# Softmax difference of a differential attention: three engines share the step that two did

## The chip, the cores and the metric

The kernel runs on one core of a Trainium2 chip. The metric is device time of one execution in microseconds (us); lower is better. The core's engines run side by side, each through its own fixed queue of instructions, and wait for one another by semaphores: TensorE (PE in the profile; its weight loads are PEld), VectorE (DVE), ScalarE (ACT), GpSimd (POOL) and SyncE (SP), which issues all transfers here.

## The reference

One layer of a streaming encoder: RMSNorm, one input projection whose columns feed an attention group and a gated convolution, an output projection, a residual and a final RMSNorm. The change concerns the attention of 2048 prompt frames, which has two softmaxes for each of 4 heads and subtracts them:

```python
def diff_attend(q, k, v, q_pos, k_pos, lam, rel_bias):
    s = jnp.einsum('bqhcd,bkhcd->bchqk', q, k, preferred_element_type=f32) * SCALE
    bias = rel_bias[rel_bucket(k_pos[None, :] - q_pos[:, None])]
    s = s + jnp.transpose(bias, (2, 0, 1)).astype(f32)[None, None]
    vis = chunk_id(k_pos)[None, :] <= chunk_id(q_pos)[:, None]
    s = jnp.where(vis, s, NEG)
    p = jax.nn.softmax(s, axis=-1)
    a = p[:, 0] - lam * p[:, 1]
    return jnp.einsum('bhqk,bkhd->bqhd', a.astype(v.dtype), v)
```

## The kernel before, in words

The frames are taken in four parts `p` of 512. For each part and head `h`, `unit_a` makes queries, keys, values and the gate by projections (`proj`, L217 is their matmul), `attend` does the attention, and `unit_c` does a quarter of the convolution. Every projection splits its weights into a high and a low half: ScalarE casts `wr` to `wh` (L196), GpSimd (VectorE for some columns) subtracts to get `wl` (L197), and three matmuls take the place of one.

`attend` goes through a part's four tiles of 128 queries, in two pairs. The keys that a tile sees (16 meta tokens and all frames up to its own) are cut into 1 to 5 chunks of at most 512 columns. There are 64 tiles and 176 chunks. For each chunk and each of the two components, `softmax_diff` does this:

- two matmuls write negated scores to PSUM (`s`, L438 and L439, three buffers),
- VectorE takes each row's minimum `nm` (L388; L385 with the bias for the last chunk),
- ScalarE writes the exponentials to SBUF (L389): component 0 to a tile `p0`, component 1 to a tile `p1` (12 and 6 buffers), and adds up each row.

Then `coefs` makes from minima and sums one factor for each row, chunk and component, `cf` (L362 to L369, small instructions on VectorE and one on ScalarE). The factor of component 1 contains minus lambda. The last loop scales both and adds them into `p0`; it is the place of the change. Back in `attend`, TensorE transposes `p0` block by block into PSUM (`pt`, L454), ScalarE casts that to `ah` (L457), VectorE subtracts to get `al` (L458), and TensorE multiplies with the values (`po`, L461 to L463). Other lines in the prediction: L297 takes the values from PSUM to SBUF before their transposes (L308), L180 is in the gate's `softplus_neg`, L532 scales a convolution input by the norm on GpSimd, L144 casts the input on ScalarE, and L686 is the matmul of the output projection, whose first half is laid among the last tiles.

The program is written head after head. A scheduler, which runs when the program is built, sets the order of each engine's queue, so that projections stand between the matmuls of the attention; a change in one place moves instructions elsewhere too.

Of the kernel before, what the change touches and what calls it, by code (L numbers as in the profile page):

```python
# [13 lines left out]
AF = mybir.ActivationFunctionType  # L14
ALU = mybir.AluOpType
# [32 lines left out]
def hybrid_step(ctx: ExitStack, tc: tile.TileContext, x, xT, ckT, cv, scT, rel_bias, norm_g, w_in,  # L48
# [10 lines left out]
    op = pool("op", 3)  # L59
# [9 lines left out]
    V, S, G, T = nc.vector, nc.scalar, nc.gpsimd, nc.tensor  # L69
# [281 lines left out]
    def coefs(nm, l, nch, pn, lam=None):  # L351

        n = nm.shape[1]
        lam = lam2 if lam is None else lam
        cf = sm.tile([P, 2, 5], F32, tag="cf", name="cf")[:pn, :n, :nch]
        r = sm.tile([P, 2], F32, tag="r2", name="r2")[:pn, :n]
        if nch == 1:
            V.reciprocal(cf, l)
            V.tensor_tensor(cf, cf, lam[:pn].unsqueeze(2), op=ALU.mult)
            return cf  # L360
        M = sm.tile([P, 2], F32, tag="M2", name="M2")[:pn, :n]
        V.tensor_reduce(M, nm, op=ALU.min, axis=AX.X)  # L362
        V.tensor_tensor(nm, nm, M.unsqueeze(2).broadcast_to([pn, n, nch]), op=ALU.subtract)
        S.activation(nm, nm, AF.Exp, scale=-1.0)
        V.tensor_tensor(l, l, nm, op=ALU.mult)
        V.tensor_reduce(M, l, op=ALU.add, axis=AX.X)
        V.reciprocal(r, M)
        V.tensor_tensor(r, r, lam[:pn], op=ALU.mult)  # L368
        V.tensor_tensor(cf, nm, r.unsqueeze(2).broadcast_to([pn, n, nch]), op=ALU.mult)  # L369
        return cf  # L370

    def softmax_diff(pn, chunks, mm, bz):


        nch = len(chunks)
        nm = sm.tile([P, 2, 5], F32, tag="nm", name="nm")[:pn, :, :nch]
        l = sm.tile([P, 2, 5], F32, tag="l", name="l")[:pn, :, :nch]
        pr = []
        for j, (c0, w) in enumerate(chunks):
            pr.append([pp.tile([P, 512], F32, tag=f"p{c}", name=f"p{c}", bufs=NP[c])[:pn, :w] for c in range(2)])  # L380
            for c in range(2):
                s = ps_s.tile([P, 512], F32, tag="s", name="s")[:pn, :w]
                mm(c, s, c0, w)
                if j == nch - 1:
                    V.tensor_tensor_reduce(s, s, bz[:, 512 - w:], 1.0, BIG, ALU.add, ALU.min,  # L385
                                           accum_out=nm[:, c, j:j + 1])
                else:
                    V.tensor_reduce(nm[:, c, j:j + 1], s, op=ALU.min, axis=AX.X)  # L388
                S.activation(pr[j][c], s, AF.Exp, bias=nm[:, c, j:j + 1], scale=-1.0, accum_out=l[:, c, j:j + 1])  # L389
        cf = coefs(nm, l, nch, pn)  # L390
        for j, (a0, a1) in enumerate(pr):
            G.tensor_scalar(a0, a0, cf[:, 0, j:j + 1], 1.0, op0=ALU.mult, op1=ALU.mult)  # L392
            V.scalar_tensor_tensor(a0, a1, cf[:, 1, j:j + 1], a0, op0=ALU.mult, op1=ALU.add)  # L393
        return [a0 for a0, _ in pr]

    def chunks_of(t):
# [28 lines left out]
    def attend(h, p, st):  # L425
# [5 lines left out]
        for b in range(2):  # L431
            tl = [4 * p + 2 * b, 4 * p + 2 * b + 1]
            aa = []
            for t in tl:
                qs = slice(P * (t - 4 * p), P * (t - 4 * p + 1))

                def mm(c, ps, col, w):
                    T.matmul(ps, lhsT=qd[c][0][:, qs], rhs=ks[c][:, col:col + w], start=True, stop=False)  # L438
                    T.matmul(ps, lhsT=qd[c][1][:, qs], rhs=ks[c][:, col:col + w], start=False, stop=True)  # L439
                ch = chunks_of(t)  # L440
                aa.append((ch, softmax_diff(P, ch, mm, st["bz"])))
# [364 lines left out]
```

## Time and profile before

| | |
|---|---|
| median of 3 runs | 1325.93 us (1325.57 to 1329.85) |
| profiled execution | 1329.5 us, of which the span from first to last instruction 1327.7 us |
| busy: TensorE, VectorE, ScalarE, GpSimd | 97%, 75%, 56%, 55% |
| granted TensorE clock | 0.99 |

In a group of instructions the profile gives the line, the engine, the operation, what is written and read, the shape and the count, then busy us, mean ns of one, the engine's idle time ahead of them, and what ended it. `(+5 forms)` means that the group has other shapes too. A line of waits reads: who waited, for whom, us in total, how many times, the longest.

### The profile page before, as it was taken

The numbers are of one execution on the slowest core, as the hardware profiler recorded it, in microseconds if no ns is written. First come the engines' busy times: TensorE is split into PE (matmuls) and PEld (weight loads), VectorE is DVE, ScalarE is ACT, GpSimd is POOL, SyncE is SP. The second block draws the span as 40 slices with busy tenths as digits, with TensorE's granted clock in tenths as the row PEclk, the third lists the DMA queues.
The fourth block names the chain that finished last, engine by engine and source line by source line (L and its number), as shares of the span: only waits on it lengthen the run. The fifth ranks groups of instructions, "written<-read, shape, count | busy, mean of one in ns | idle before, by whom it ended". The sixth has DMA issues, their size and how long they took to land.

```text
span 1327.7 us, 21145 instructions
## 1 busy us (share of the span) xinstructions
PE 1281.4 (97%) x7058; PEld 1105.9 (83%) x7058; DVE 1000.8 (75%) x2086; ACT 740.3 (56%) x1854; POOL 732.1 (55%) x659
## 2 busy tenths in 40 slices
PE   8999999999899999999999999999999999999897
PEld 6999999978788887888888887878888888888675
DVE  7756667657798858898969867788788897856653
ACT  6645453564556547566655565565656675654221
POOL 5675655556466665466656745566567575543100
PEclk9999999999999999899999999999999999999999
DMA  9743533764334447444353453444334434567741
GB/s 296 214 146 95 161 90 97 221 212 151 113 111 136 144 136 234 155 135 143 97 167 115 140 183 103 120 137 126 103 105 152 143 120 137 165 196 255 223 159 52
DMA packets 108045, 198.72 MB, mean 150 GB/s; under 512 B 17408, under 2 KB 45600, under 8 KB 107936
## 3 DMA queue, kind: packets, MB, share of 16 engines
q1 hardware_dynamic: 107936, 197.37, 48.0%
q8 instruction: 55, 0.90, 0.3%
q14 instruction: 54, 0.44, 0.1%
HBM read 145.62 MB, written 43.26 MB: 142 GB/s over the span
## 4 chain that ended last, share of the span: by engine, by line
PE 69%; DVE 17%; ACT 5%; DMA 4%; issue 3%; POOL 1%; SPq 1%; DVEq 0%; ACTq 0%; POOLq 0%
PE pj L217 40%; PE po L686 9%; PE pt L454 3%; PE s L438 3%; PE s L439 3%; DVE p L393 3%; PE po L462 2%; PE po L463 2%; PE po L461 2%; DMA out<-y 2%; DVE nm L388 2%; ACT p L389 1%; DMA xt<-in_xT 1%; DVE al L458 1%; ACT wh L196 1%
## 5 line engine op out<-in xcount | busy, mean ns | idle before, releaser
L197 POOL TENSOR_TENSOR wl<-wr,wh 128x512 fp32r<-128x512 f32 x240 | 329.7, 1378 | 258.1 <-ACT wh L196 248.2
L217 PE MATMUL pj<-xh,wh 128*128 128x512 f32 (+2 forms) x1280 | 459.1, 360 | 5.9 <-DVE r L368 2.4
L217 PE MATMUL pj<-xl,wh 128*128 128x512 f32 (+2 forms) x1280 | 456.7, 357 | 0.7 <-DVE xl L145 0.7
L217 PE MATMUL pj<-xh,wl 128*128 128x512 f32 (+2 forms) x1280 | 455.4, 356 | 0.0
L389 ACT ACTIVATE p<-s,nm 128x384 f32<-128x384 f32 (+5 forms) x352 | 208.9, 596 | 156.9 <-DVE nm L388 112.2
L217 PEld LDWEIGHTS pj<-xh,wh 128*128 128x128 f32 x1280 | 244.6, 191 | 37.5 <-issue 2.7
L217 PEld LDWEIGHTS pj<-xh,wl 128*128 128x128 f32 x1280 | 244.1, 191 | 30.9 <-issue 1.1
L217 PEld LDWEIGHTS pj<-xl,wh 128*128 128x128 f32 x1280 | 244.4, 191 | 30.3 <-DVE xl L145 1.4
L196 ACT CAST wh<-wr 128x512 fp32r<-128x512 f32 x256 | 157.2, 617 | 99.5 <-PE pj L217 70.2
L393 DVE SCALAR_TENSOR_TENSOR p<-p,cf,p 128x384 f32<-128x384 f32 (+5 forms) x176 | 168.5, 984 | 16.1 <-POOL p L392 15.1
L392 POOL TENSOR_SCALAR p<-p,cf 128x384 f32<-128x384 f32 (+5 forms) x176 | 122.7, 713 | 56.3 <-DVE cf L369 40.8
L438 PE MATMUL s<-ks,q 128*128 128x384 f32 (+5 forms) x352 | 128.8, 368 | 5.3 <-ACT p L389 5.3
L388 DVE TENSOR_REDUCE nm<-s 128x1 f32<-128x384 f32 (+3 forms) x224 | 122.6, 559 | 14.9 <-PE s L439 14.6
L458 DVE TENSOR_TENSOR al<-pt,ah 128x512 fp32r<-128x512 f32 x144 | 97.2, 683 | 38.1 <-ACT ah L457 37.5
L439 PE MATMUL s<-ks,q 128*128 128x384 f32 (+5 forms) x352 | 122.7, 350 | 2.0 <-DMA q<-q 2.0
L666 POOL TENSOR_TENSOR cll<-ct,chh 128x512 fp32r<-128x512 f32 x40 | 54.5, 1368 | 112.1 <-ACT chh L664 108.3
L457 ACT CAST ah<-pt 128x512 fp32r<-128x512 f32 x144 | 80.8, 587 | 44.3 <-PE pt L454 41.3
L454 PE MATMUL pt<-ident,p 128*128 128x128 f32 x544 | 86.1, 273 | 4.3 <-DVE p L393 4.3
L462 PE MATMUL po<-al,vh 128*128 128x256 f32 x288 | 83.2, 289 | 2.9 <-DVE al L458 2.8
L385 DVE CUSTOM_DVE_ANT_0 s<-s,bz 128x512 f32<-128x512 f32 (+5 forms) x128 | 73.8, 588 | 12.8 <-PE s L439 10.2
L461 PE MATMUL po<-ah,vh 128*128 128x256 f32 x288 | 81.7, 284 | 0.0
L463 PE MATMUL po<-ah,vl 128*128 128x256 f32 x288 | 81.1, 282 | 0.0
(238 smaller groups left out, 2200.1 us busy)
## 6 DMA issues: line engine op xcount, KB each, us to landing
wr<-in_w_in SPq DMA_DIRECT2D x128, 512.0 KB, 3.7
ct<-cat SPq DMA_DIRECT2D x28, 512.0 KB, 4.7
q<-q SPq DMA_DIRECT2D x64, 128.0 KB, 3.4
out<-y SPq DMA_DIRECT2D x32, 256.0 KB, 3.5
ks<-ksd SPq DMA_DIRECT2D x8, 776.0 KB, 6.1
xr<-in_x SPq DMA_DIRECT2D x24, 256.0 KB, 5.1
out<-g SPq DMA_DIRECT2D x24, 256.0 KB, 3.0
xt<-in_xT SPq DMA_DIRECT2D x24, 256.0 KB, 4.5
```

The source lines that it names most:

```text
L196: S.copy(wh, wi)
L197: (V if (col in (CQ, CK) if p == 0 else col in (CQ, CZ)) else G).tensor_tensor(wl, wi, f32(wh), op=ALU.subtract)
L217: T.matmul(ps, lhsT=a[:, k % 4], rhs=b[k][:, b0:b1], start=(k == 0 and i == 0), stop=(k == KT - 1 and i == 2))
L388: V.tensor_reduce(nm[:, c, j:j + 1], s, op=ALU.min, axis=AX.X)
L389: S.activation(pr[j][c], s, AF.Exp, bias=nm[:, c, j:j + 1], scale=-1.0, accum_out=l[:, c, j:j + 1])
L392: G.tensor_scalar(a0, a0, cf[:, 0, j:j + 1], 1.0, op0=ALU.mult, op1=ALU.mult)
L393: V.scalar_tensor_tensor(a0, a1, cf[:, 1, j:j + 1], a0, op0=ALU.mult, op1=ALU.add)
L438: T.matmul(ps, lhsT=qd[c][0][:, qs], rhs=ks[c][:, col:col + w], start=True, stop=False)
L439: T.matmul(ps, lhsT=qd[c][1][:, qs], rhs=ks[c][:, col:col + w], start=False, stop=True)
L454: T.transpose(pt[:, i, P * qi:P * (qi + 1)], cols(aa[qi], NM + P * (2 * j + i), P), ident)
L458: V.tensor_tensor(al, pt, f32(ah), op=ALU.subtract)
L686: T.matmul(ps, lhsT=a[k][:, :rows], rhs=b[k], start=(k == 0 and i == 0), stop=(k == KT - 1 and i == 2))
```

## The change

```diff
         cf = coefs(nm, l, nch, pn)
         for j, (a0, a1) in enumerate(pr):
-            G.tensor_scalar(a0, a0, cf[:, 0, j:j + 1], 1.0, op0=ALU.mult, op1=ALU.mult)
-            V.scalar_tensor_tensor(a0, a1, cf[:, 1, j:j + 1], a0, op0=ALU.mult, op1=ALU.add)
+            S.activation(a0, a0, AF.Copy, scale=cf[:, 0, j:j + 1])
+            V.tensor_scalar(a1, a1, cf[:, 1, j:j + 1], None, op0=ALU.mult)
+            G.tensor_tensor(a0, a0, a1, op=ALU.add)
         return [a0 for a0, _ in pr]
```

`G`, `V` and `S` are GpSimd, VectorE and ScalarE. Before, GpSimd scaled component 0 in place, and VectorE multiplied component 1 by its factor and added, in one instruction. Now ScalarE scales component 0 (L392) and VectorE component 1 (L393), each in place, and GpSimd adds the two (L394). Lines below move down by one: the transposes are now L455, the products L462 to L464, the output projection L687.

What the scheduler makes of it is shown at three places. First VectorE's queue at the last tile of part 2, head 3 (four chunks), before:

```order
L369 TENSOR_TENSOR cf_9797<-nm_9747,r2_9798 128x2x4
L559 TENSOR_TENSOR g_10753<-pj_10765,g_10749 128x512
L393 SCALAR_TENSOR_TENSOR p0_9749<-p1_9750,cf_9797,p0_9749 128x400
L393 SCALAR_TENSOR_TENSOR p0_9761<-p1_9762,cf_9797,p0_9761 128x384
L388 TENSOR_REDUCE nm_10122<-s_10138 128x1
L393 SCALAR_TENSOR_TENSOR p0_9773<-p1_9774,cf_9797,p0_9773 128x384
L393 SCALAR_TENSOR_TENSOR p0_9785<-p1_9786,cf_9797,p0_9785 128x384
L388 TENSOR_REDUCE nm_10122<-s_10143 128x1
```

and now:

```order
L369 TENSOR_TENSOR cf_9901<-nm_9851,r2_9902 128x2x4
L393 TENSOR_SCALAR p1_9854<-p1_9854,cf_9901 128x400
L393 TENSOR_SCALAR p1_9866<-p1_9866,cf_9901 128x384
L393 TENSOR_SCALAR p1_9878<-p1_9878,cf_9901 128x384
L393 TENSOR_SCALAR p1_9890<-p1_9890,cf_9901 128x384
L388 TENSOR_REDUCE nm_10230<-s_10239 128x1
L388 TENSOR_REDUCE nm_10230<-s_10246 128x1
```

The four now stand together behind the factors; the next tile's minima (L388) no longer stand between them.

Second, ScalarE's queue at the same tile, now (before, no such scaling is in it, and the next tile's exponentials L389 follow on L364 at once):

```order
L364 ACTIVATE nm_9851<-nm_9851 128x2x4
L392 ACTIVATE p0_9853<-p0_9853,cf_9901 128x400
L473 COPY o_9590<-po_9708 128x256
L474 ACTIVATE o_9591<-po_9708 128x256
L392 ACTIVATE p0_9865<-p0_9865,cf_9901 128x384
L392 ACTIVATE p0_9877<-p0_9877,cf_9901 128x384
L392 ACTIVATE p0_9889<-p0_9889,cf_9901 128x384
L196 CAST wh_10975<-wr_10969 128x512
L389 ACTIVATE p1_10233,l_10231<-s_10239,nm_10230 128x400
```

The scalings stand ahead of the next weight cast and the next tile's exponentials. In GpSimd's queue the four adds stand where the four scalings stood.

Third, TensorE's queue in the last pair of tiles of all, from the transposes to the first products with the values, before:

```order
L454 MATMUL pt_13264<-ident_100,p0_13167 128x128
L454 MATMUL pt_13264<-ident_100,p0_13110 128x128
L454 MATMUL pt_13264<-ident_100,p0_13179 128x128
L686 MATMUL po_14028<-woh4_13562,chh_14022 128x512
L686 MATMUL po_14028<-woh4_13562,cll_14023 128x512
L686 MATMUL po_14028<-wol4_13570,chh_14022 128x512
```

and now:

```order
L455 MATMUL pt_13440<-ident_100,p0_13338 128x128
L455 MATMUL pt_13440<-ident_100,p0_13277 128x128
L455 MATMUL pt_13440<-ident_100,p0_13350 128x128
L687 MATMUL po_14393<-ks0_14274,cs_14380 128x512
L462 MATMUL po_13424<-ah_13430,vh_12944 128x256
L463 MATMUL po_13424<-al_13431,vh_12944 128x256
L464 MATMUL po_13424<-ah_13430,vl_12945 128x256
```

Before, 22 matmuls of the output projection followed on the transposes ahead of the first product (L461); now one does.

## The prediction

> **What bounds the kernel now.** First the page: busy times, then the chain.
>
> ```profile
> span 1327.7 us, 21145 instructions
> ...
> PE 1281.4 (97%) x7058; PEld 1105.9 (83%) x7058; DVE 1000.8 (75%) x2086; ACT 740.3 (56%) x1854; POOL 732.1 (55%) x659
> ...
> PE 69%; DVE 17%; ACT 5%; DMA 4%; issue 3%; POOL 1%; SPq 1%; DVEq 0%; ACTq 0%; POOLq 0%
> ```
>
> TensorE is busy nearly always, and the change leaves its 7058 matmuls alone. Only its waits can move: 1327.7 − 1281.4 = 46 us, plus what hides in pipelined matmuls. Next, the stretch from 60 to 1100 us, which holds most of the attention, and what TensorE waits for in it:
>
> ```profile
> core 0: us, PE busy (x) PEld busy (x) DVE busy (x) ACT busy (x) POOL busy (x), PEclk, DMA share, GB/s
> ...
> 60.00:1100.00 1040.00, 1012.94 (x5690) 881.93 (x5689) 812.68 (x1656) 603.56 (x1502) 630.61 (x562) 0.99 0.45 137
> ```
> ```profile
> PE s L438 <- ACT p L389: 5.3, 8, 3.3
> PE pt L454 <- DVE p L393: 4.3, 4, 2.5
> PE ptv L308 <- DVE g L297: 3.9, 4, 2.2
> PE po L462 <- DVE al L458: 2.8, 3, 1.7
> PE pj L217 <- DVE r L368: 2.4, 2, 1.2
> ...
> PE po L686 <- DVE g L687: 1.9, 1, 1.9
> PE pj L217 <- DVE g L344: 1.6, 1, 1.6
> PE pts L504 <- DVE as L499: 1.5, 1, 1.5
> ```
> ```profile
> ACT p L389 <- DVE nm L388: 106.9, 96, 3.9
> ...
> ACT p L389 <- DVE nm L385: 28.9, 35, 2.7
> ```
>
> The columns of a wait are total us, times and longest. VectorE ends nearly all of them. The one row that names ScalarE (5.3 us for the exponentials) leads back to VectorE: ScalarE itself stood still for 106.9 and 28.9 us there until VectorE had the minima. GpSimd ends none. So VectorE, 78% busy in this stretch (812.68 of 1040), makes TensorE late, and the change takes work from it.
>
> **The change part by part.** Removed are GpSimd's scaling (L392) and VectorE's fused multiply-add (L393), 176 each:
>
> ```profile
> L393 DVE SCALAR_TENSOR_TENSOR p<-p,cf,p 128x384 f32<-128x384 f32 (+5 forms) x176 | 168.5, 984 | 16.1 <-POOL p L392 15.1
> L392 POOL TENSOR_SCALAR p<-p,cf 128x384 f32<-128x384 f32 (+5 forms) x176 | 122.7, 713 | 56.3 <-DVE cf L369 40.8
> ```
>
> VectorE loses 176 × 984 ns = 173 us, GpSimd 176 × 713 ns = 125 us.
>
> *VectorE gains* 176 scalings of one SBUF tile by a column. The nearest rows are L180, the same operation with constants:
>
> ```profile
> L180 DVE TENSOR_SCALAR g<-g 128x512 f32<-128x512 f32 x24 | 16.4, 684 | 0.2
> ...
> L180 DVE TENSOR_SCALAR g<-g 128x272 f32<-128x272 f32 x16 | 9.3, 583 | 0.4
> ```
> ```profile
> L180 DVE TENSOR_SCALAR g<-g x40: 296/447/1518, 41.0 to 1084.2; 128x512 f32<-128x512 f32 x24, 128x272 f32<-128x272 f32 x16
> ```
> ```profile
> L393 DVE SCALAR_TENSOR_TENSOR p<-p,cf,p x176: 369/935/1784, 47.0 to 1173.8; 128x384 f32<-128x384 f32 x64, 128x400 f32<-128x400 f32 x44, 128x512 f32<-128x512 f32 x44, 128x272 f32<-128x272 f32 x16
> ```
> ```profile
> L458 DVE TENSOR_TENSOR al<-pt,ah x144: 674/682/693, 55.2 to 1200.5; 128x512 fp32r<-128x512 f32 x144
> ```
>
> The chunks are about 400 wide. Between 583 ns at 272 and 684 ns at 512 that is 637 ns, or 112 us in all: VectorE saves 61 us. Ends: at the median 447 ns it pays 79 us and saves 94; if the scaling takes the 984 ns of the old instruction it saves nothing. I take the mean because these spreads (296 to 1518 ns, 369 to 1784 ns) come with the place of the operands: L458, which reads one operand from PSUM, varies by 19 ns only. In the example below two L393 take 3.30 us exactly while GpSimd has its 2.85 us of wl.
>
> The Trainium skill ("SBUF — State Buffer", section "Who interferes with whom") explains such spreads: VectorE and GpSimd share one port pair, locked for a whole instruction, by VectorE where it reads two SBUF tensors or runs a two-port mode. The trace agrees so far. By that rule the new scaling still locks and can be held for a whole add; if that happened to every one, the saving would be zero, which is the second case below.
>
> *GpSimd gains* 176 additions. The same operation is L532:
>
> ```profile
> L532 POOL TENSOR_TENSOR g<-g,rb 128x512 f32<-128x512 f32 x12 | 16.2, 1352 | 3.4 <-PE pj L217 1.2 <-PE pt L454 1.1 <-DVE g L531 1.0
> ...
> L532 POOL TENSOR_TENSOR g<-g,rb 128x280 f32<-128x280 f32 x8 | 7.4, 930 | 3.6 <-DVE g L531 3.6
> ```
> ```profile
> L197 POOL TENSOR_TENSOR wl<-wr,wh 128x512 fp32r<-128x512 f32 x240 | 329.7, 1378 | 258.1 <-ACT wh L196 248.2
> ```
>
> At 400 wide: 930 + 422 × 120/232 = 1148 ns, 202 us in all, 77 us more than it loses; 55% busy becomes 61%. This costs nothing by itself: behind GpSimd's queue stand the wl subtractions for the projections, and before these it idled 258.1 us for ScalarE, cover for three times the increase; without it, each add would push a wl and so a projection by 1.15 us.
>
> *ScalarE gains* 176 copies scaled by a column:
>
> ```profile
> L389 ACT ACTIVATE p<-s,nm 128x384 f32<-128x384 f32 (+5 forms) x352 | 208.9, 596 | 156.9 <-DVE nm L388 112.2
> ```
> ```profile
> L144 ACT ACTIVATE xh<-xt,ng 128x512 fp32r<-128x512 f32 x24 | 16.5, 724 | 7.6 <-DMA xt<-in_xT 7.6
> ```
>
> L389 has these widths and takes 596 ns: 105 us. L144, which is scaled from SBUF at 512, bounds it above at 127 us. ScalarE goes from 56% to 64%. In its order the scalings of a tile come in one run ahead of the next tile's exponentials: four make 2.4 us.
>
> *The path from the coefficients to the transposes.* A tile of four chunks:
>
> ```profile
> 845.51 0.17 DVE L369 TENSOR_TENSOR cf<-nm,r 128x8 f32<-128x8 f32 x1
> 845.78 2.90 POOL L392 TENSOR_SCALAR p<-p,cf 128x400 f32<-128x400 f32 x4 [0.92 <-DVE cf L369]
> ...
> 846.65 1.58 DVE L393 SCALAR_TENSOR_TENSOR p<-p,cf,p 128x400 f32<-128x400 f32 x2
> ...
> 848.61 3.30 DVE L393 SCALAR_TENSOR_TENSOR p<-p,cf,p 128x384 f32<-128x384 f32 x2
> 848.64 2.85 POOL L197 TENSOR_TENSOR wl<-wr,wh 128x512 fp32r<-128x512 f32 x2
> ```
>
> From 845.68 to 851.91: 6.2 us. Now one copy (0.6) and four adds (4 × 1.15) make 5.2 us, and 6.6 us if a wl of 1.38 us is in GpSimd when the first add is ready. So this path stays as it was; its wait of 4.3 us (pt) passes to GpSimd and may be 3 to 6: I add 0.5. The six buffers of p1, now freed by the add, come free as early as before, so the exponentials that wait for them lose nothing.
>
> *What VectorE's relief gives.* Of the 61 us, 156/176, the share of L393 that the stretch holds, fall into it:
>
> ```profile
> 60.00:1100.00 1040.00, 149.31 (x156) 0.99 0.45 137
> ```
>
> That is 54 us over 64 tiles, 0.85 us a tile. A wait shrinks by it only where the saved work stood between; I take half, 0.43 us, times the waits of the rows above without L393's (8 + 4 + 3 + 2 + 1 + 1 + 1 = 20): 8.6 us, of which the shortest waits lack some, so −8. Ends: 0, and −16 for the whole 0.85 us.
>
> *ScalarE's longer queue*: the s wait (5.3 us, 8 times) gets 0 to 4 us; I take +1, since ScalarE spends most of its idle time waiting for VectorE.
>
> *The new order on TensorE.* In the last pair of tiles one matmul instead of 22 separates the transposes from the products. The trace has the work between:
>
> ```profile
> 1175.15 0.82 PE L454 MATMUL pt<-ident,p 128*128 128x128 f32 x6
> ...
> 1177.37 1.07 ACT L457 CAST ah<-pt 128x512 fp32r<-128x512 f32 x2
> ...
> 1177.98 1.29 DVE L458 TENSOR_TENSOR al<-pt,ah 128x512 fp32r<-128x512 f32 x2 [1.78 <-ACT ah L457]
> ```
>
> Transposes end at 1175.97, the first al at about 1178.6: 2.6 us, formerly covered. At its shortest (half of 1.07 and of 1.29) it is 1.2 us. I take +2.
>
> Loading and the tail cost nothing: no L392 or L393 is there.
>
> Sum: −8 + 0.5 + 1 + 2 = −4.5 us. The profiled execution took 1329.5 us (span 1327.7 and 1.8 around it), 3.6 us over the median of 1325.93; set against the median the sum gives **1321.4 us**.
>
> **The rivals.**
> - *No change.* The relief falls where nobody waits, or the shared operands cost VectorE what it saves (the lower end above). For it: only 20 us of named waits are VectorE's. Against: they end on instructions queued behind L393. Half the relief, −4, with the 3.5 us of costs: 1325.4 us (1322 to 1330 by the ends of both).
> - *Slower, by GpSimd.* The transposes now wait for an engine whose queue holds instructions of 1.38 us. If two wl stand before the adds, the path of a tile grows from 6.2 to 8 us. It decides from the point where that excess, 1.8 us, passes the slack ahead of the transposes. The slack so far:
>
> ```profile
>   DVE p L393: 9.7, 8
> ```
>
>  This is what TensorE's loads and matmuls for pt idled, in 8 places, so 56 or more of the 64 tiles had some. If a third of the 64 loses half of it, 0.9 us, that is +19, less the relief of 8 and with the other 3 us of costs: 1340 us. The Trainium skill ("GPSIMD Engine Reference", section "Engine selection") has a rule that speaks for it: elementwise additions belong on VectorE, GpSimd being about half as fast with two inputs.
> - *Slower, by ScalarE.* The 2.4 us run of scalings delays exponentials and so the PSUM buffers of the scores: 20 more waits like those of L438 (0.66 us each): +13, less the relief of 8 and with the other 2.5: 1333 us.
>
> **How the numbers follow.** Faster by the sum 0.42, its own range 1312 (relief −16, costs 2) to 1322; no change 0.32; slower by GpSimd 0.18, by ScalarE 0.08. About 0.3% (4 us) is what a measurement of this kernel tells from no change, so these are the three chances: 0.42, 0.32, 0.26. The range 1311 to 1340 leaves out one in ten on the slow side and the few cases where hidden stalls go too.
>
> **What would show it.** Right: VectorE near 940 us, GpSimd near 810, ScalarE near 845; the new L393 near 640 ns, L394 near 1150, L392 near 600; the waits on L297, L458 and L368 shorter; a wait of pt on L394 of 3 to 6 us. Wrong: L393 near 900 ns; pt waiting more than 10 us on GpSimd; s L438 waiting far over 5.3 us on ScalarE; or pj waiting for wl, which it now never does.

## The result: 0.66% slower, and the profile after

The changed kernel takes 1336.76 us (median; 1335.76 to 1339.62), the kernel before, beside it on the same chip, 1327.87 us. The ratio is 1.0066, 95% interval 1.0041 to 1.0091: +8.9 us, where the prediction had −4.5. The page of the changed kernel's profile, its span, busy times and chain:

```profile
span 1335.5 us, 21628 instructions
...
PE 1283.7 (96%) x7058; PEld 1105.7 (83%) x7058; DVE 996.5 (75%) x2086; ACT 827.3 (62%) x2030; POOL 786.6 (59%) x659
...
PE 47%; DVE 17%; ACT 5%; DMA 3%; issue 3%; POOL 0%; SPq 0%; DVEq 0%; ACTq 0%; POOLq 0%
```

GpSimd gained 54 us and ScalarE 87, somewhat less than forecast (77 and 105), but VectorE, which should have lost 61 us, lost 4 (1000.8 to 996.5). The groups of the three new instructions, and of three old ones, after:

```profile
L394 POOL TENSOR_TENSOR p<-p,p 128x384 f32<-128x384 f32 (+5 forms) x176 | 196.2, 1138 | 73.2 <-ACT p L392 48.5 <-DVE p L393 22.1 <-DVE x L109 1.4
L393 DVE TENSOR_SCALAR p<-p,cf 128x384 f32<-128x384 f32 (+5 forms) x176 | 115.8, 711 | 2.2
L392 ACT ACTIVATE p<-p,cf 128x384 f32<-128x384 f32 (+5 forms) x176 | 98.9, 622 | 51.4 <-DVE cf L369 48.5 <-DVE cf L359 2.6
L180 DVE TENSOR_SCALAR g<-g 128x512 f32<-128x512 f32 (+1 forms) x40 | 31.1, 777 | 0.8
L368 DVE TENSOR_TENSOR r<-r,lam 128x2 f32<-128x2 f32 x52 | 26.8, 515 | 1.4
L549 DVE TENSOR_SCALAR g<-g,cw 128x512 f32<-128x512 f32 (+1 forms) x16 | 17.7, 1107 | 0.0
```

The same three old ones before (L549 was L548):

```profile
L180 DVE TENSOR_SCALAR g<-g 128x512 f32<-128x512 f32 (+1 forms) x40 | 25.8, 644 | 0.6
L368 DVE TENSOR_TENSOR r<-r,lam 128x2 f32<-128x2 f32 x52 | 20.9, 402 | 1.3
L548 DVE TENSOR_SCALAR g<-g,cw 128x512 f32<-128x512 f32 (+1 forms) x16 | 9.9, 617 | 0.0
```

L393 fell by 52.7 us (168.5 to 115.8). The saving is there, and it was given back by instructions that the change does not touch: 19 us by these three groups alone. All three read and write SBUF only. L459, the old L458 with an operand in PSUM, stayed at 682 ns (683 before). Over all groups (count times mean, added up) the 784 instructions of VectorE that touch PSUM take 442.7 us before and 442.4 after; the other 1126, without L393, take 492.3 and 532.2. The timeline of the tile whose queues the section on the change shows, now:

```profile
845.88 1.29 POOL L555 TENSOR_TENSOR g<-g,rb 128x512 f32<-128x512 f32 x1 [0.76 <-DVE M L366]
845.91 0.17 DVE L367 RECIPROCAL r<-M 128x2 f32<-128x2 f32 x1
846.11 1.08 DVE L368 TENSOR_TENSOR r<-r,lam 128x2 f32<-128x2 f32 x1
847.22 0.17 DVE L369 TENSOR_TENSOR cf<-nm,r 128x8 f32<-128x8 f32 x1
847.42 0.63 ACT L392 ACTIVATE p<-p,cf 128x400 f32<-128x400 f32 x1 [3.92 <-DVE cf L369]
847.43 2.23 DVE L393 TENSOR_SCALAR p<-p,cf 128x400 f32<-128x400 f32 x4
...
848.13 4.33 POOL L394 TENSOR_TENSOR p<-p,p 128x400 f32<-128x400 f32 x4 [0.96 <-ACT p L392]
```

L368 multiplies two numbers a row and takes 1.08 us: it ends at 847.19, and GpSimd's addition L555, which was under way, ends at 847.17. From the coefficients (847.39) to the last addition (852.46) it is 5.1 us, as worked out in the prediction.

TensorE's waits after, over the whole execution (columns: total us, times, longest):

```profile
PE po L463 <- DVE al L459: 6.2, 6, 2.4
PE s L439 <- ACT p L389: 5.9, 7, 1.6
PE po L687 <- DVE y L688: 5.9, 5, 2.6
PE ptv L308 <- DVE g L297: 5.5, 3, 2.7
...
PE pt L455 <- DVE pt L450: 2.4, 2, 1.3
PE pj L217 <- ACT p L389: 2.3, 1, 2.3
...
PE po L687 <- ACT ks L650: 1.0, 1, 1.0
...
PE po L462 <- ACT ah L458: 0.7, 1, 0.7
...
PE po L687 <- DVE cs L667: 0.4, 1, 0.4
PE pt L455 <- POOL p L394: 0.3, 1, 0.3
```

The wait of the transposes on L394 is 0.3 us. Added up, all rows of this view make 43.0 us, before 38.2. With TensorE's busy time (1281.4 to 1283.7) that is +7.1 of the +7.8 us between the two spans. No single wait carries it: al for the products grew most (2.8 to 6.2), several small ones are new.

### The profile page after: what moved, and what is told of

It reads as the page before. It is cut to its first block, busy times and chain, and to the rows that moved or that the text cites. A ratio compares the mean times of both kernels' runs of the same rounds, so it can differ in the third digit from the quotient of the medians.

```text
span 1335.5 us, 21628 instructions
## 1 busy us (share of the span) xinstructions
PE 1283.7 (96%) x7058; PEld 1105.7 (83%) x7058; DVE 996.5 (75%) x2086; ACT 827.3 (62%) x2030; POOL 786.6 (59%) x659
## 4 chain that ended last, share of the span: by engine, by line
PE 47%; DVE 17%; ACT 5%; DMA 3%; issue 3%; POOL 0%; SPq 0%; DVEq 0%; ACTq 0%; POOLq 0%
PE pj L217 23%; PE po L687 8%; PE pt L455 3%; DVE p L393 3%; PE s L439 3%; PE s L440 3%; PE po L463 2%; PE po L464 2%; PE po L462 2%; DVE nm L388 2%; ACT p L389 1%; DVE r L368 1%; DVE al L459 1%; DMA out<-y 1%; DVE l L365 1%
## 5 line engine op out<-in xcount | busy, mean ns | idle before, releaser
L197 POOL TENSOR_TENSOR wl<-wr,wh 128x512 fp32r<-128x512 f32 x240 | 321.5, 1345 | 215.4 <-ACT wh L196 174.6
L389 ACT ACTIVATE p<-s,nm 128x384 f32<-128x384 f32 (+5 forms) x352 | 208.8, 596 | 101.5 <-DVE nm L388 61.2
L394 POOL TENSOR_TENSOR p<-p,p 128x384 f32<-128x384 f32 (+5 forms) x176 | 196.2, 1138 | 73.2 <-ACT p L392 48.5
L388 DVE TENSOR_REDUCE nm<-s 128x1 f32<-128x384 f32 (+3 forms) x224 | 120.9, 558 | 16.7 <-PE s L440 15.9
L392 ACT ACTIVATE p<-p,cf 128x384 f32<-128x384 f32 (+5 forms) x176 | 98.9, 622 | 51.4 <-DVE cf L369 48.5
L459 DVE TENSOR_TENSOR al<-pt,ah 128x512 fp32r<-128x512 f32 x144 | 97.3, 682 | 40.8 <-ACT ah L458 40.7
L393 DVE TENSOR_SCALAR p<-p,cf 128x384 f32<-128x384 f32 (+5 forms) x176 | 115.8, 711 | 2.2
L458 ACT CAST ah<-pt 128x512 fp32r<-128x512 f32 x144 | 81.0, 584 | 38.7 <-PE pt L455 38.0
L455 PE MATMUL pt<-ident,p 128*128 128x128 f32 x544 | 89.1, 275 | 2.9 <-DVE pt L450 2.4
L462 PE MATMUL po<-ah,vh 128*128 128x256 f32 x288 | 81.9, 284 | 0.7 <-ACT ah L458 0.7
```

Of the source, the lines that this page charges most:

```text
L197: (V if (col in (CQ, CK) if p == 0 else col in (CQ, CZ)) else G).tensor_tensor(wl, wi, f32(wh), op=ALU.subtract)
L393: V.tensor_scalar(a1, a1, cf[:, 1, j:j + 1], None, op0=ALU.mult)
L394: G.tensor_tensor(a0, a0, a1, op=ALU.add)
L455: T.transpose(pt[:, i, P * qi:P * (qi + 1)], cols(aa[qi], NM + P * (2 * j + i), P), ident)
L459: V.tensor_tensor(al, pt, f32(ah), op=ALU.subtract)
```

## The experiments

Two things changed at once: the work of three engines, and, through the scheduler, the order of every queue. So most experiments hold all queues to the order of a named kernel, by edges between neighbours that order instructions and add no wait, and change the work alone. Instructions that the named kernel has no place for are left free. Three theories stood against one another at first: A, the additions on GpSimd cost the time, through transposes that come late or a VectorE that is held; B, the new order costs it, whatever the work; C, ScalarE's longer queue costs it.

```python
for a, b in zip(row, row[1:]):
    tc.add_manual_dep(b, a.name, edge, reason="pin")
```

Each ratio is to the kernel before, timed beside it in five rounds.

**1. The new work in the order of before.** The diff of the change, and the order of before; the scalings on ScalarE are free.

> The new three instructions, with the queues of TensorE, VectorE, GpSimd and SyncE, and ScalarE's but for the 176 new scalings, held in the order of the kernel before (order edges between neighbours, no waits). Theory A (operands shared between GpSimd and VectorE: the longer adds hold other VectorE instructions, so VectorE stays near 995 us busy): 1.004 to 1.009 times before. Theory B (the scheduler's new order bares waits on TensorE): 0.998 to 1.002. Theory C (ScalarE's 105 us of scalings delay exponentials and casts): 1.004 to 1.009, with more wait of TensorE on ScalarE than the 5.9 us in the changed kernel.

Measured: 1.0198 (1.0182 to 1.0215), outside the ranges of all three theories. In this order the transposes do wait for GpSimd, as the second rival had it, though 5.4 us and not 19:

```profile
PE po L463 <- DVE al L459: 8.1, 7, 3.0
...
PE s L439 <- ACT p L389: 5.7, 7, 1.6
PE pt L455 <- POOL p L394: 5.4, 4, 3.0
```
```profile
PE 1288.6 (95%) x7058; PEld 1110.0 (82%) x7058; DVE 958.5 (71%) x2086; ACT 826.1 (61%) x2030; POOL 783.9 (58%) x659
...
L394 POOL TENSOR_TENSOR p<-p,p 128x384 f32<-128x384 f32 (+5 forms) x176 | 191.5, 1103 | 169.0 <-DVE p L393 105.1
```

VectorE is relieved by 42 us here (1000.8 to 958.5), and the kernel is slower all the same. The scalings stand where the fused instructions stood, among the next tile's minima, and the additions wait 105 us for them (22 us in the changed kernel).

So the scheduler's new order spares the new work 1.3%; what that order costs by itself, the next run tells.

**2. The old work in the order of after.** No edit but the order; the scalings and the fused instruction are free.

> The two instructions of before, with all other instructions held in the order of the changed kernel. Theory A: 0.998 to 1.002 times before. Theory B: 1.004 to 1.009, about the changed kernel's 1.0066. Theory C: 0.998 to 1.002. If order and instructions each carry half, both this run and the one with the orders exchanged lie near 1.003.

Measured: 1.0061 (1.0047 to 1.0074). The kernel before, doing nothing new, gets as slow in this order as the changed kernel is. Its longest waits:

```profile
PE po L686 <- DVE y L687: 8.8, 5, 3.3
PE s L438 <- ACT p L389: 8.3, 6, 2.1
PE pt L454 <- DVE pt L449: 4.6, 4, 2.8
```

The sum of all its rows is 43.6 us, 5.4 over before. As with the changed kernel the new waits are many and short, in other places than there.

**3. A narrow addition.** The order of after; only one column of each chunk is added, and the rest of the second softmax is left out.

```diff
-            G.tensor_tensor(a0, a0, a1, op=ALU.add)
+            G.tensor_tensor(a0[:, :1], a0[:, :1], a1[:, :1], op=ALU.add)
```

> The changed kernel in its own order, but GpSimd adds one column of each chunk instead of all (the second softmax is left out of the other columns), so that each add takes about 0.1 us instead of 1.14. It also frees the transposes from the add, but they waited 0.3 us for it in all. Theory A: VectorE falls from 996 us to 930 to 960, with the factor products (515 ns) and L180 (936 ns at 512) back at or under their means of before, and the time to 0.990 to 1.000 times before. Theory B: VectorE may fall, but the time stays at 1.004 to 1.008. Theory C: the same as B.

Measured: 0.9929 (0.9915 to 0.9942). Its busy times and L393:

```profile
PE 1276.0 (97%) x7058; PEld 1102.2 (84%) x7058; DVE 939.2 (71%) x2086; ACT 827.6 (63%) x2030; POOL 634.0 (48%) x659
...
L393 DVE TENSOR_SCALAR p<-p,cf 128x384 f32<-128x384 f32 (+5 forms) x176 | 81.7, 517 | 2.2
```

This is VectorE's relief as the prediction meant it, and it is large: VectorE at 939 us (forecast: near 940), and 1.3% less time than the old work in the same order (GpSimd is lighter too, 634 us). ScalarE carries all of its new load here and costs no visible time. The free scalings stand at the same places of ScalarE's queue as in the changed kernel. So the whole difference between 0.9929 and 1.0066 is the price of the full additions (a narrow one still takes 251 ns, not the 0.1 us expected). The three groups L180, L368 and L549 come to 65.5 us here, 56.6 before and 75.6 in the changed kernel: about half of their growth comes with the full additions. Theories A and B are both right in part: the order alone costs 0.6%, and the additions 1.4%.

**4. Only ScalarE's part.** ScalarE scales component 0, VectorE keeps the fused instruction, GpSimd does nothing; the scheduler's own order.

```diff
-            G.tensor_scalar(a0, a0, cf[:, 0, j:j + 1], 1.0, op0=ALU.mult, op1=ALU.mult)
+            S.activation(a0, a0, AF.Copy, scale=cf[:, 0, j:j + 1])
             V.scalar_tensor_tensor(a0, a1, cf[:, 1, j:j + 1], a0, op0=ALU.mult, op1=ALU.add)
```

> One part alone: ScalarE scales component 0, VectorE keeps the fused multiply-add, GpSimd has nothing in this step; the scheduler orders it anew. Theory A: GpSimd's 125 us of scaling are gone, so L393 falls from 984 ns to 750 to 850 and VectorE to 950 to 975 us, and the time is 0.990 to 1.000 times before. Theory B says only that a new order may cost up to 1% whatever the work. Theory C: ScalarE carries the same 99 us as in the changed kernel, so 1.004 to 1.009.

Measured: 0.9917 (0.9901 to 0.9933), 1315.12 us. This version beats both kernels, and theory C falls: ScalarE does here what it does in the changed kernel. Its busy times and its unchanged fused instruction:

```profile
PE 1274.5 (97%) x7058; PEld 1102.7 (84%) x7058; DVE 970.1 (74%) x2086; ACT 823.6 (63%) x2030; POOL 600.0 (46%) x483
...
L393 DVE SCALAR_TENSOR_TENSOR p<-p,cf,p 128x384 f32<-128x384 f32 (+5 forms) x176 | 131.5, 776 | 20.3 <-ACT p L392 19.5
```

VectorE lost 31 us although none of its instructions changed: L393 takes 776 ns instead of 984. GpSimd has 132 us less to do beside it; that this is the reason, experiments 6 and 11 show, where GpSimd gets work back in this order and VectorE comes to 1006.9 and 1003.3 us.

**5. The wide addition off the path.** As 3, and behind each narrow addition GpSimd adds p1 to itself at full width.

```diff
+            G.tensor_tensor(a1, a1, a1, op=ALU.add)
```

> As the third experiment (GpSimd adds one column of each chunk; the rest of the second softmax is left out), in the changed kernel's order, but at the place of the wide add GpSimd also adds p1 to itself, 176 full-width additions. GpSimd's load and the time at which a p1 buffer comes free are those of the changed kernel; only p0, which the transposes read, does not wait for the wide add. If the add hurts by lengthening the way from the coefficients to the transposes (theory 'path'): ratio to the kernel before near the 0.993 of the narrow add, 0.991 to 0.997, VectorE near 990 us busy and the p wait of the transposes gone. If it hurts by GpSimd's load, by VectorE being held behind two-input adds or by late p1 buffers (theory 'load'): 1.003 to 1.009, near the changed kernel's 1.0066, with VectorE near 995 us and po waiting for al some 5 us.

Measured: 0.9962 (0.9949 to 0.9976), in the range of the path. But VectorE came out at 959.9 us, not near 990: this addition reads one tile twice, took 896 ns and held VectorE less than the changed kernel's (L393: 536 ns). Experiment 12 has an addition of two tiles in its place.

**6. Additions that nobody needs.** Experiment 4 in its own order, with the same addition behind each fused instruction.

> As the fourth experiment (ScalarE scales, VectorE keeps the fused multiply-add), in that kernel's order, with an addition of p1 to itself on GpSimd behind each fused multiply-add: 176 full-width additions that nobody's data needs, but p1 is freed only behind them. Theory 'load': the gain of 0.8% goes, 0.999 to 1.010, VectorE's instructions with SBUF operands are longer (L393 from 755 ns to 850 or more). Theory 'path': 0.990 to 0.995, as without the additions (0.9917).

Measured: 1.0013 (0.9998 to 1.0027), against 0.9917 without.

```profile
PE 1282.7 (96%) x7058; PEld 1103.8 (83%) x7058; DVE 1006.9 (76%) x2086; ACT 824.0 (62%) x2030; POOL 780.8 (59%) x659
...
L393 DVE SCALAR_TENSOR_TENSOR p<-p,cf,p 128x384 f32<-128x384 f32 (+5 forms) x176 | 146.8, 863 | 19.8 <-ACT p L392 19.1
```

The same VectorE instructions in the same order take 36.8 us longer, and the kernel 0.96%, for work on GpSimd whose result is not used. Since p1 is freed behind the addition, later buffers may have a part in it.

**7. Experiment 4's work in the order of before.**

> ScalarE scales, VectorE keeps the fused multiply-add, and all other instructions stand in the order of the kernel before; only the 176 scalings, now on ScalarE, are placed freely. It tells whether the fourth experiment's 0.9917 comes from the work or from the order that the scheduler made for it. Work: 0.989 to 0.995. Order: 0.998 to 1.005. Beside the first experiment (same order, scalings on ScalarE too, but multiply and add on two engines, 1.0198) it gives the price of splitting the fused instruction at this order: 2 to 3% by work, under 2% by order.

Measured: 1.0084 (1.0066 to 1.0103). The same work takes 1.7% more than in its own order. The scores wait for the exponentials twice as long as before (5.3 us):

```profile
PE s L438 <- ACT p L389: 11.0, 13, 3.3
```

That the scalings on ScalarE alone make this wait is not shown: in experiment 1, with the same scalings in nearly the same queue of ScalarE, it is 5.7 us.

**8. Two lines swapped.** The kernel before, with the same work.

```diff
-            S.copy(o32[:, 256 * b:256 * (b + 1)], po)
             S.activation(sq[:, 256 * b:256 * (b + 1)], po, AF.Square)
+            S.copy(o32[:, 256 * b:256 * (b + 1)], po)
```

> The kernel before with two neighbouring lines of attend swapped (the square on ScalarE is written ahead of the copy, both from the same PSUM tile): the same instructions, in another order by the scheduler. It measures how much such a reordering alone moves the time. If order is a lottery of half a per cent (theory 'order'): 0.994 or less or 1.006 or more is possible, and the changed kernel's 1.0066 need not be the work. If order matters little: 0.998 to 1.002.

Measured: 1.0047 (1.0030 to 1.0064), between the two theories' bounds: a swap of two neighbours moved the scheduler's result by half a per cent.

**9, 10, 11. Work and order crossed.** The new work in experiment 4's order (additions free), experiment 4's work in the order of after (scalings free), and the old work in experiment 4's order (scalings free).

> The changed kernel's three instructions in the order of the fourth experiment (0.9917): VectorE's scaling stands where that kernel has its fused multiply-add, the additions on GpSimd are placed freely. Theory 'the split and the add cost by themselves' (1.1% in before's order: 1.0198 against 1.0084): 0.999 to 1.007. Theory 'order alone' (the fourth experiment is fast because of its order): 0.990 to 0.995.

> The fourth experiment's two instructions (ScalarE scales, VectorE multiplies and adds at the place of the changed kernel's scaling) in the changed kernel's order; GpSimd adds nothing. Theory 'the split and the add cost': about 1.1% under the changed kernel's 1.0066, 0.991 to 0.998. Theory 'order alone': 1.003 to 1.009.

> The two instructions of the kernel before (GpSimd scales, VectorE multiplies and adds) in the order of the fourth experiment; the scalings on GpSimd are placed freely. Theory 'that order is better for any work': 0.990 to 0.996. Theory 'an order fits the work for which it was made': 1.000 to 1.010.

Measured: 0.9957 (0.9940 to 0.9974), 1.0210 (1.0188 to 1.0232), 0.9963 (0.9939 to 0.9986). With the runs above:

| work \ order | of before | of after | of experiment 4 |
|---|---|---|---|
| old | 1 | 1.0061 | 0.9963 |
| new (the change) | 1.0198 | 1.0066 | 0.9957 |
| experiment 4's | 1.0084 | 1.0210 | 0.9917 |

In two of the three orders the change of work alone makes no difference (1.0066 to 1.0061, 0.9957 to 0.9963), and in the order of before it costs 2%. Experiment 4's work beats the old work only in its own order; in the other two it is 0.8% and 1.5% slower. The 1.0210 was outside both expectations. There the fused instructions stand in VectorE's queue right behind the coefficients, a place made for scalings that wait for nothing, and each holds the queue until ScalarE is done:

```profile
L393 DVE SCALAR_TENSOR_TENSOR p<-p,cf,p 128x384 f32<-128x384 f32 (+5 forms) x176 | 116.9, 708 | 55.0 <-ACT p L392 54.5
```

VectorE's busy time, 970.9 us, is the third lowest of the table's nine, and the kernel is the slowest; experiment 1 has the lowest, 958.5, and is the next slowest. So the engine's sum does not rank these kernels. TensorE's waits, added up, nearly do: 29.0 us in experiment 4, 38.1 before, 52.5 in experiment 1, 59.8 in experiment 10. They are not the whole difference: TensorE's busy time for the same 7058 matmuls rises with them (1274.5, 1281.4, 1288.6 and 1293.3 us), and the granted clock falls (0.993, 0.990, 0.986, 0.983). Of experiment 4's gain of 0.83%, 0.37 comes with its order (0.9963), 0.46 with its work.

**12. A two-tile addition off the path.** As 5, with `G.tensor_tensor(a1, a1, a0, op=ALU.add)` as the wide addition.

> As the fifth experiment (narrow additions into p0, in the changed kernel's order; the rest of the second softmax is left out), but the wide addition off the path now reads two tiles, p1 <- p1 + p0, as the changed kernel's does, instead of one tile twice. In the fifth experiment it took 896 ns instead of 1138, and VectorE's scaling stayed at 536 ns instead of 711. Theory 'a two-tile add holds VectorE, and that costs the time': addition near 1140 ns, L393 650 to 730 ns, VectorE 985 us or more, ratio 1.002 to 1.008, near the changed kernel's 1.0066. Theory 'path' (only p0's being late costs): ratio 0.994 to 0.998, near the fifth experiment's 0.9962, even if L393 is longer.

Measured: 1.0001 (0.9986 to 1.0016), between the theories.

```profile
PE 1280.6 (96%) x7058; PEld 1104.8 (83%) x7058; DVE 975.3 (73%) x2086; ACT 826.8 (62%) x2030; POOL 821.8 (62%) x835
...
L395 POOL TENSOR_TENSOR p<-p,p 128x384 f32<-128x384 f32 (+5 forms) x176 | 191.0, 1096 | 5.3
L393 DVE TENSOR_SCALAR p<-p,cf 128x384 f32<-128x384 f32 (+5 forms) x176 | 88.0, 553 | 2.2
```

In the order of after, then: 0.9929 with narrow additions, 1.0001 with full ones beside them, 1.0066 when the transposes must wait for the full ones. What comes with the load costs 0.7%, and what comes with the place on the path another 0.65%. Two limits: GpSimd does 35 us more here than in the changed kernel, so the first share is rather too large; and L393 is 553 ns here and 711 there, so the second holds not only p0's lateness but also VectorE's being held longer (975 to 996 us). The two were not taken apart.

## Why the prediction was wrong, step by step

- *What bounds it*: right. TensorE is busy to 96%, its waits on VectorE and, through VectorE, on ScalarE decide, and GpSimd ended 0.3 us of them.
- *The three prices*: near. L393 711 ns (forecast 637, between its ends of 447 and 984), L394 1138 (1148), L392 622 (596). ScalarE came to 827 us (845), GpSimd to 787 (810).
- ***VectorE's relief, −8: the first term that failed.*** The step "VectorE saves 61 us" took the saving of one group for a relief of the engine. L393 saved 52.7 us and VectorE 4.3. GpSimd's 176 instructions now take 196 us instead of 123, and VectorE's other instructions on SBUF grew by 40 us: 492 us before, 506 in experiment 3 (this order, narrow additions), 532 with the full ones. So some 14 us come with the order and 26 with the full additions. The text had this mechanism, but held it only against the new L393 and, as a lower end, as a rival; it belonged to every VectorE instruction without a PSUM operand. The next step, from less work on VectorE to shorter waits, failed too: in experiment 1 VectorE is relieved by 42 us and the kernel is 2% slower. With narrow additions there is a gain (experiment 3 against 2: −1.3%, 17.5 us, with less on GpSimd and no transposes behind full additions), and what comes with the load (12 against 3: +9.6 us) and with the place (the changed kernel against 12: +8.6 us) of the full ones takes it back. So the exchange of work, −6.5 in the sum (−8, +0.5, +1), is worth +0.7 us at the new order (1.0066 against 1.0061; the intervals leave about 4 us either way), −0.8 at experiment 4's and +26 at the old one.
- *The path, +0.5*: its length was right, and the forecast wait of 3 to 6 us on L394 did not come (0.3). The wait that grew is that of the products for al, and its two longest pieces (2.43 and 2.20 us of 6.2) are not p0's lateness: the transposes had ended 12 and 10 us before. The longest:

```profile
404.42 3.49 DVE L393 TENSOR_SCALAR p<-p,cf 128x272 f32<-128x272 f32 x3
...
407.83 0.68 DVE L459 TENSOR_TENSOR al<-pt,ah 128x512 fp32r<-128x512 f32 x1
...
408.57 0.58 PE L463 MATMUL po<-al,vh 128*128 128x256 f32 x1 [2.43 <-DVE al L459]
```

  Three scalings of a later tile stand ahead of al in VectorE's queue. Experiment 3, in the same order, has this wait too (2.4 us), so it comes with the order.
- *ScalarE, +1*: near, 5.3 to 5.9 us, and 5.7 with the same work in the old order (experiment 1).
- ***The new order, +2: the second term that failed.*** In the last pair of tiles it was near: the first products' waits for ah and al make 1.1 us, and the output projection's for ks and cs right behind them 1.4. But only that place was priced. Over the whole program the order costs 0.61%, 8.1 us (experiment 2), in many short waits. The scalings ahead of al are one decision of the scheduler that can be named; for most of the sum it is open which one makes it.
- *The rivals*: "no change" named what became of the work, and "slower, by GpSimd" the sign, by another way: not by transposes that wait visibly, but by GpSimd's load and by an order of which the text priced one place. With +8.1 for the order and +0.7 for the work the two parts make the measured +8.9 but for rounding, because the second is what the first leaves. Taken work first they are +26 and −17.5 (1.0198, then 1.0066): work and order do not add, and no split between them is the only one.

The Trainium skill ("SBUF — State Buffer", section "Who interferes with whom") describes the lock on the port pair that VectorE and GpSimd share; the trace agrees, with +36.8 us on VectorE for additions that nobody needs (experiment 6).

## What to carry to other kernels

Where work goes from VectorE to GpSimd, price it by VectorE's sum over all instructions that touch SBUF alone, not by the group that gets shorter, and do not take that sum for time: with 42 us less on VectorE experiment 1 was 2% slower. ScalarE's scalings took 622 ns with and without the additions, and with GpSimd left out that version gained 0.83% in its own order, 0.46% of it by the work; in the other two orders it lost. Where a scheduler sets the order, an edit of the work is also a draw of an order worth about half a per cent either way: time the old work in the new order before explaining a difference of that size.

## What was not expected of the hardware

A VectorE instruction of two numbers a row can last as long as an instruction of GpSimd. All 52 of L368, after:

```profile
L368 DVE TENSOR_TENSOR r<-r,lam x52: 147/162/1277, 61.3 to 1184.3; 128x2 f32<-128x2 f32 x52
```

Their median is 162 ns and their longest 1277 ns, and this one stands on the way from the sums to the coefficients. All 21 that take over 600 ns end 15 to 20 ns after an instruction of GpSimd on SBUF that was under way (wl and others; none is one of the new additions). And an addition of 384 columns on GpSimd takes, at its shortest, 820 ns when it reads one tile twice (experiment 5; 822 in experiment 6) and 997 when it reads two (experiment 12): here the second tile costs some 175 ns. The means are less clear, 896 and 1039 ns for one tile and 1096 for two.
